# A transformer block's first loads: the eight norm columns by GpSimd's queue, the first x chunk by halves, its weights by ScalarE's queue, the table later, and a fixed order of two chunks

## The chip, the cores and the metric

The kernel runs on one core of one Trainium2 chip. The metric is the device time of one execution, in microseconds (us), as the median over executions. A profile of one more execution shows what each engine did: TensorE (PE, with PEld for its weight loads), VectorE (DVE), ScalarE (ACT), GpSimd (POOL), and SyncE (SP), which here only issues transfers. A "q" behind an engine's name is its instruction sequencer, which issues DMAs.

## What is computed

One block of a transformer on 512 tokens of width 1024, in float32. The parts that matter here:

```
h = rmsnorm(x, attn_pre_g)          # x * rsqrt(mean(x*x)) * g
proj = h @ w_in                     # split into q, k, v, gates of two attentions
k_cmp, v_cmp = compress_kv(...)     # two small MLPs on strided windows
o = [nsa_attention(...), swa_attention(..., sinks)]
x = x + rmsnorm(o @ w_o, attn_post_g)
h = rmsnorm(x, mlp_pre_g)
a, u = split(h @ w_gate_up);  y = (gelu(conv(a)) * u) @ w_down
x = x + rmsnorm(y, mlp_post_g)
x = x + (p @ w_ple) * sigmoid(x @ w_ple_gate)
```

## The kernel before

Tokens lie along the free dimension: x is kept transposed, as 8 chunks of 128 rows (features) by 512 columns (tokens). Each float32 product is made of three matmuls with operands that are split in a rounded high part and a rest, low part: high by high, high by low, low by high. So each weight and each activation is split first: ScalarE (or VectorE) makes the high part by a copy in the rounded type, VectorE subtracts it for the low part.

The program starts with `consts`: a table `cols` of 128 by 160 float32 (norm gains, convolution taps, sinks and more as columns) is loaded through ScalarE's DMA queue; small constants are set by GpSimd; a first activation loads ScalarE's function table; VectorE zeroes a tile, and TensorE runs `WARM` matmuls on it, which compute nothing that is used.

`load_x` then issues from SyncE's queue, chunk by chunk, x (256 KB) and the first weights `wv` (204 KB, 408 columns: three value projections and the gates). For each chunk ScalarE multiplies x with the norm gain, a column of the table, and rounds it to the high part (line 330); the high part of the weights is made on VectorE for chunk 0 (line 332) and on ScalarE for the others (line 334); VectorE makes both low parts (lines 335, 336); and the squares of x are summed on the side for the norm (lines 321 to 325), whose factor is applied after the products. These instructions carry `keep`, which holds them in the order of the program on their engine.

`v_natural` runs 96 matmuls on these: for each of 8 chunks and each of 4 blocks of 128 tokens the three terms, into four PSUM banks. x is the stationary operand (loaded as weights of TensorE), `wv` the moving one. Lines 356 to 358 are high by high, high by low and low by high. Behind them come the compress projections, which use the same x tiles.

`bias_tables` builds distance tables for the attentions; it also negates the eight sink columns of the table (line 295), long before they are used.

The order of instructions on an engine is laid out when the kernel is built, by a list scheduler that simulates the program and starts what is ready; `keep_in_program_order` fixes the order of marked instructions. Fillers (projections that are not urgent) are put between the steps of the attentions. Weight tiles rotate in few buffers: tag "wh" has 6, and the raw weights 2.

Of the kernel before, what the change touches and what calls it, by code (L numbers as in the profile page):

```python
# [26 lines left out]
C_GPRE, C_GPOST, C_GMLP, C_GMPOST = 0, 8, 16, 24  # L27
C_CW = 32
C_CB = C_CW + 3 * NFF
C_SINK = C_CB + NFF  # L30
# [18 lines left out]
HALF = [slice(h * H, (h + 1) * H) for h in range(2)]  # L49
# [3 lines left out]


FILL_STEP = 650.0
WARM = 9
RATES = [0.36, 0.36, 0.9, 0.6]
BORDER = {6: .36, 7: .7, 8: .9}
SIX = 4
# [5 lines left out]
class Block:  # L65
# [181 lines left out]
    def consts(self):  # L247
        nc, cp = self.nc, self.cp
        self.cols = cp.tile([P, NCOL], F32, name="cols")
        nc.scalar.dma_start(self.cols, self.io["cols"])  # L250
        self.ones = cp.tile([P, 1], F32, name="ones")
        nc.gpsimd.memset(self.ones, 1.0)
        self.mhalf = cp.tile([P, NQT], F32, name="mhalf")
        nc.gpsimd.memset(self.mhalf, -0.5)
        first = self.tiny([P, 1], "act")
        nc.scalar.activation(first, self.ones, AF.Copy)
        idle = self.s([P, T], F32R)
        nc.vector.memset(idle.bitcast(F32), 0.0)
        warm = self.ps("mm")
        for i in range(WARM):  # L260
            nc.tensor.matmul(warm, idle[:, 0:P], idle, start=True, stop=True)
        self.ident = cp.tile([P, P], F32, name="ident")
        nc.gpsimd.memset(self.ident, 1.0)
        nc.gpsimd.affine_select(out=self.ident, in_=self.ident, compare_op=ALU.is_equal, fill=0.0, base=0,
                                pattern=[[-1, P]], channel_multiplier=1)
# [4 lines left out]
    def bias_tables(self):  # L270

        self.phase = "biastables"
        nc = self.nc
        fr = nc.gpsimd.to_reg(BIG)
        it = self.s([P, T], I32)
        nc.gpsimd.iota(it, pattern=[[-1, T]], base=T - P, channel_multiplier=1)
        dist = self.u([P, 7 * P])
        self.dist = dist[:, :T]
        nc.vector.tensor_copy(self.dist, it)
        nc.gpsimd.affine_select(out=self.dist, in_=self.dist, compare_op=ALU.is_ge, fill=fr, base=T - P,  # L280
                                pattern=[[-1, T]], channel_multiplier=1)
# [12 lines left out]
        self.nsink = self.cp.tile([P, 8], F32, name="nsink")  # L294
        nc.vector.tensor_scalar(self.nsink, self.cols[:, C_SINK : C_SINK + 8], -1.0, None, op0=ALU.mult)
        self.qscale = self.cp.tile([P, 8], F32, name="qscale")
        for h in range(16):
            sl = SLOPES[8 + h if h < 8 else h - 8]
            nc.gpsimd.memset(self.qscale[h % 2 * 64 : h % 2 * 64 + 64, h // 2 : h // 2 + 1], -(HD ** -0.5) / sl)


    def load_x(self):
        self.phase = "loadx"
        nc = self.nc
        self.xg = []
        self.wv = []
        acc = self.s([P, T])
        keep = self.tc.keep_in_program_order
        raws = []
        for c in range(KC):  # L310
            if c % 2 == 0:
                x2 = self.u([P, 2, T], F32, "p")
            xt = x2[:, c % 2, :]
            keep(nc.sync.dma_start(xt, self.io["xT"][:, c, :]))
            wr = self.u([P, 408])
            keep(nc.sync.dma_start(wr, self.io["wv"][c]))
            raws.append((xt, wr))

        def squares(c):
            if c == 0:  # L320
                keep(nc.scalar.activation(acc, raws[0][0], AF.Square))
            else:
                sq = self.s([P, T])
                keep(nc.scalar.activation(sq, raws[c][0], AF.Square))
                keep(nc.vector.tensor_add(acc, acc, sq))

        for c, (xt, wr) in enumerate(raws):
            g = self.u([P, 2, T], F32R)
            hi, lo = (self.u([P, 408], F32R, "wh") for _ in range(2))
            keep(nc.scalar.activation(g[:, 0, :], xt, AF.Copy, scale=self.col(C_GPRE + c)))  # L330
            if c == 0:
                keep(nc.vector.tensor_copy(hi, wr))
            else:
                keep(nc.scalar.activation(hi, wr, AF.Copy))
            keep(nc.vector.tensor_sub(lo, wr, hi.bitcast(F32)))
            keep(nc.vector.scalar_tensor_tensor(g[:, 1, :], xt, self.col(C_GPRE + c), g[:, 0, :].bitcast(F32),
                                                op0=ALU.mult, op1=ALU.subtract))
            self.wv.append((hi, lo))
            self.xg.append(g)
            if c > 0:  # L340
                squares(c - 1)
        squares(KC - 1)
        self.xacc = acc

    def v_natural(self):
        self.phase = "vnatural"
        nc = self.nc
        NV = 408
        pv = [self.ps(t) for t in ("s", "s", "s", "o")]
        for c in range(KC):  # L350
            x = self.xg[c]
            hi, lo = self.wv[c]
            for tb in range(NQT):
                ts = slice(tb * P, (tb + 1) * P)
                o = pv[tb][:, :NV]
                nc.tensor.matmul(o, x[:, 0, ts], hi, start=c == 0, stop=False)
                nc.tensor.matmul(o, x[:, 0, ts], lo, start=False, stop=False)
                nc.tensor.matmul(o, x[:, 1, ts], hi, start=False, stop=c == KC - 1)
        self.r1c, self.r1b = self.rstd(self.xacc, "r1")
        self.vs = []  # L360
        self.gate = self.cp.tile([P, NQT, 24], F32, name="gate")
        for tb in range(NQT):
            v = self.s([P, T])
            nc.scalar.activation(v[:, :NV], pv[tb][:, :NV], AF.Copy, scale=self.r1c[:, tb : tb + 1])
            vt = self.u([P, 6, 2, HD], F32R)
            vv = v[:, : 6 * HD].rearrange("p (k d) -> p k d", k=6)
            nc.vector.tensor_copy(vt[:, :, 0, :], vv)
            nc.vector.tensor_sub(vt[:, :, 1, :], vv, vt[:, :, 0, :].bitcast(F32))
            self.vs.append(vt)
            e = self.tiny([P, 24], "ge")  # L370
# [838 lines left out]
```

## Time and profile before

| | us |
|---|---|
| median of 3 runs | 665.4 (665.25 to 665.5) |
| the profiled execution | 665.88 |
| its span, first to last instruction | 663.9 |

The span covers the instructions of the core; the profiled execution's own time is 2.0 us longer, and lies 0.48 us above the median. In the rows, times are microseconds from the start of the span unless marked ns, L330 is line 330 of the kernel, and "out<-in" names the tiles that an instruction writes and reads. The ends of matmuls are modelled: matmuls are pipelined, so the distance between the starts of two says more than their duration.

### The profile page before, as it was taken

The numbers are of one execution on the slowest core, as the hardware profiler recorded it, in microseconds if no ns is written. First come the engines' busy times: TensorE is split into PE (matmuls) and PEld (weight loads), VectorE is DVE, ScalarE is ACT, GpSimd is POOL, SyncE is SP. The second block draws the span as 40 slices with busy tenths as digits, with TensorE's granted clock in tenths as the row PEclk, the third lists the DMA queues.
The fourth block names the chain that finished last, engine by engine and source line by source line (L and its number), as shares of the span: only waits on it lengthen the run. The fifth ranks groups of instructions, "written<-read, shape, count | busy, mean of one in ns | idle before, by whom it ended". The sixth has DMA issues, their size and how long they took to land.

```text
span 663.9 us, 9247 instructions
## 1 busy us (share of the span) xinstructions
PE 656.2 (99%) x3297; PEld 552.9 (83%) x3297; DVE 399.8 (60%) x828; ACT 324.0 (49%) x602; POOL 168.3 (25%) x247
## 2 busy tenths in 40 slices
PE   9999999999999999999999999999999999999997
PEld 8988778888888888888888888888888888889986
DVE  7795887978856469586555555555542333323873
ACT  7454587978887566264333333333332223222351
POOL 1111597677486060021101010111100000001000
PEclk9999999999999999999999999999999999999999
DMA  8436621202273430112233333323323444332032
GB/s 301 169 109 202 187 65 48 59 22 66 63 231 141 136 128 31 65 64 96 95 97 99 100 102 96 106 98 98 96 87 88 119 132 129 88 95 88 3 111 80
DMA packets 25069, 69.55 MB, mean 105 GB/s; under 512 B 3136, under 2 KB 5184, under 8 KB 25024
## 3 DMA queue, kind: packets, MB, share of 16 engines
q1 hardware_dynamic: 24880, 68.89, 33.0%
q8 instruction: 26, 0.43, 0.3%
q14 instruction: 19, 0.16, 0.1%
q10 hardware_dynamic: 144, 0.08, 0.0%
HBM read 59.52 MB, written 2.10 MB: 93 GB/s over the span
## 4 chain that ended last, share of the span: by engine, by line
PE 93%; DVE 3%; ACT 2%; POOL 1%; issue 0%; DMA 0%; SPq 0%; ACTq 0%; DVEq 0%
PE mlpup_pss L145 4%; PE mlpup_pss L149 4%; PE mlpup_pss L148 4%; PE mlpup_psmm L145 3%; PE mlpup_pst L145 3%; PE mlpup_psmm L149 3%; PE mlpup_pst L149 3%; PE mlpup_pst L148 3%; PE mlpup_psmm L148 3%; PE mlpdown_pss L149 3%; PE mlpdown_pss L145 3%; PE mlpdown_pss L148 3%; PE nsa_pso L555 2%; PE nsa_pst L522 2%; PE mlpdown_psmm L145 2%; PE mlpdown_psmm L149 2%
## 5 line engine op out<-in xcount | busy, mean ns | idle before, releaser
L126 ACT ACTIVATE mlpup_wh<-mlpup_wr 128x1024 fp32r<-128x1024 f32 x38 | 40.3, 1061 | 78.6 <-PE mlpup_pss L148 43.3
L982 POOL TENSOR_TENSOR mlpup_s<-mlpup_s,r3b 128x512 f32<-128x512 f32 x22 | 29.5, 1343 | 186.8 <-ACT mlpup_s L981 186.8
L126 ACT ACTIVATE mlpdown_wh<-mlpdown_wr 128x1024 fp32r<-128x1024 f32 (+1 forms) x28 | 28.0, 1000 | 84.6 <-PE mlpdown_pss L148 30.1
L130 DVE TENSOR_TENSOR mlpdown_wh<-mlpdown_wr,mlpdown_wh 128x1024 fp32r<-128x1024 f32 (+1 forms) x28 | 32.8, 1170 | 60.2 <-ACT mlpdown_wh L126 60.2
L130 DVE TENSOR_TENSOR mlpup_wh<-mlpup_wr,mlpup_wh 128x1024 fp32r<-128x1024 f32 x38 | 47.0, 1238 | 5.1 <-ACT mlpup_wh L126 5.0
L145 PE MATMUL mlpup_pss<-r_u,mlpup_wh 128*128 128x512 f32 x120 | 46.8, 390 | 0.0
L148 PE MATMUL mlpup_pss<-r_u,mlpup_wh 128*128 128x512 f32 x120 | 46.7, 389 | 0.0
L149 PE MATMUL mlpup_pss<-r_u,mlpup_wh 128*128 128x512 f32 x120 | 46.7, 389 | 0.0
L545 POOL TENSOR_SCALAR nsa_u<-nsa_u,nsa_nrc,gate 128x512 f32<-128x512 f32 (+3 forms) x64 | 38.4, 613 | 16.9 <-DVE nsa_nrc L681 11.7
L647 ACT ACTIVATE nsa_u<-nsa_u,nsa_nnm 128x512 f32<-128x512 f32 (+3 forms) x64 | 35.4, 554 | 7.6 <-DVE nsa_nnm L640 7.4
L527 DVE TENSOR_TENSOR nsa_u<-nsa_pst,nsa_u 128x512 fp32r<-128x512 f32 (+1 forms) x43 | 29.4, 686 | 6.8 <-ACT nsa_u L524 6.5
L237 POOL TENSOR_TENSOR mlpdown_s<-mlpdown_s,mlpdown_s 128x512 f32<-128x512 f32 x6 | 7.8, 1302 | 100.3 <-ACT mlpdown_s L236 100.3
L130 POOL TENSOR_TENSOR fill_wh<-fill_wr,fill_wh 128x1024 fp32r<-128x1024 f32 (+2 forms) x14 | 26.9, 1924 | 24.1 <-ACT fill_wh L126 21.5
L975 DVE TENSOR_TENSOR mlpup_u<-mlpup_pss,r3b 128x512 f32<-128x512 f32 x17 | 11.7, 691 | 34.4 <-PE mlpup_pss L149 34.4
L981 ACT ACTIVATE mlpup_s<-mlpup_s 128x512 f32<-128x512 f32 x22 | 13.8, 632 | 37.7 <-DVE mlpup_s L980 37.6
L149 PE MATMUL mlpdown_pss<-mlpup_u,mlpdown_wh 128*128 128x512 f32 (+1 forms) x88 | 32.0, 364 | 0.0
L145 PE MATMUL mlpdown_pss<-mlpup_u,mlpdown_wh 128*128 128x512 f32 (+1 forms) x88 | 32.0, 364 | 0.0
L148 PE MATMUL mlpdown_pss<-mlpup_u,mlpdown_wh 128*128 128x512 f32 (+1 forms) x88 | 31.9, 363 | 0.0
L145 PE MATMUL mlpup_pst<-r_u,mlpup_wh 128*128 128x512 f32 x80 | 31.1, 389 | 0.0
L148 PE MATMUL mlpup_pst<-r_u,mlpup_wh 128*128 128x512 f32 x80 | 31.1, 389 | 0.0
L149 PE MATMUL mlpup_pst<-r_u,mlpup_wh 128*128 128x512 f32 x80 | 31.1, 389 | 0.0
L145 PE MATMUL mlpup_psmm<-r_u,mlpup_wh 128*128 128x512 f32 x80 | 31.1, 389 | 0.0
(426 smaller groups left out, 1988.1 us busy)
## 6 DMA issues: line engine op xcount, KB each, us to landing
mlpup_wr<-in_gu_dram SPq DMA_DIRECT2D x38, 512.0 KB, 3.3
mlpdown_wr<-in_down_dram SPq DMA_DIRECT2D x16, 512.0 KB, 3.6
fill_wr<-in_win_dram SPq DMA_DIRECT2D x6, 512.0 KB, 4.0
mlpdown_wr<-in_down_dram SPq DMA_DIRECT2D x8, 384.0 KB, 3.1
fill_u<-fill_u SPq DMA_DIRECT2D x20, 128.0 KB, 2.6
loadx_u<-in_xT_dram SPq DMA_DIRECT2D x8, 256.0 KB, 4.9
compress_u<-projk_u SPq DMA_DIRECT2D x16, 128.0 KB, 2.3
mlpdown_wr<-in_wpg_dram SPq DMA_DIRECT2D x4, 512.0 KB, 3.4
```

Source lines behind the costliest of these rows:

```text
L126: h = nc.scalar.activation(hi, raw, AF.Copy)
L130: l = eng.tensor_sub(lw, raw, hi.bitcast(F32))
L145: r = self.pin(mm(ps, hi, x[:, 0, :], start=start, stop=False))
L148: mm(ps, lo, x[:, 0, :], start=False, stop=False)
L149: mm(ps, hi, x[:, 1, :], start=False, stop=stop)
L522: self.att(nc.tensor.transpose(pt[:, r * P : (r + 1) * P], src, self.ident))
L527: nc.vector.tensor_sub(t[rs, part, :], pt[rs], t[rs, 0, :].bitcast(F32))
L545: self.nc.gpsimd.tensor_scalar(ap, ap, col, gate, op0=ALU.mult, op1=ALU.mult)
L555: self.att(nc.tensor.matmul(po, v, t[:, part, :], start=start, stop=stop))
L647: nc.scalar.activation(dst, dst, AF.Exp, bias=nm[:, r, b : b + 1], scale=-1.0, accum_out=sm[:, r, b : b + 1])
L981: nc.scalar.activation(c0, c0, AF.Gelu_apprx_tanh)
L982: nc.gpsimd.tensor_mul(c0, c0, self.r3)
```

## The change

The eight columns of the first norm get a tile of their own, `gpre`, which GpSimd's queue loads; the scaling of x reads it. The whole table is loaded from SyncE's queue, behind the weights of chunk 2. The weights of chunk 0 are loaded from ScalarE's queue, where the table was. The x of chunk 0 comes in two halves of 256 columns, and is scaled and split by halves. The sinks are negated by GpSimd and not by VectorE. The warm matmuls are 7 and not 9, on a zero tile of 128 columns that each reads four times. The V matmuls run by term and then by block, and those of the first two chunks are held in the order of the program.

```
--- before.py
+++ after.py
@@ -53,7 +53,7 @@
 
 
 FILL_STEP = 650.0
-WARM = 9
+WARM = 7
 RATES = [0.36, 0.36, 0.9, 0.6]
 BORDER = {6: .36, 7: .7, 8: .9}
 SIX = 4
@@ -247,18 +247,22 @@
     def consts(self):
         nc, cp = self.nc, self.cp
         self.cols = cp.tile([P, NCOL], F32, name="cols")
-        nc.scalar.dma_start(self.cols, self.io["cols"])
+        self.gpre = cp.tile([P, KC], F32, name="gpre")
+        nc.gpsimd.dma_start(self.gpre, self.io["cols"][:, C_GPRE : C_GPRE + KC])
         self.ones = cp.tile([P, 1], F32, name="ones")
         nc.gpsimd.memset(self.ones, 1.0)
         self.mhalf = cp.tile([P, NQT], F32, name="mhalf")
         nc.gpsimd.memset(self.mhalf, -0.5)
+        self.wv0 = self.u([P, 408])
+        nc.scalar.dma_start(self.wv0, self.io["wv"][0])
         first = self.tiny([P, 1], "act")
         nc.scalar.activation(first, self.ones, AF.Copy)
-        idle = self.s([P, T], F32R)
+        idle = self.s([P, P], F32R)
         nc.vector.memset(idle.bitcast(F32), 0.0)
         warm = self.ps("mm")
         for i in range(WARM):
-            nc.tensor.matmul(warm, idle[:, 0:P], idle, start=True, stop=True)
+            nc.tensor.matmul(warm.rearrange("p (a n) -> p a n", a=4), idle,
+                             idle[:, None, :].broadcast_to([P, 4, P]), start=True, stop=True)
         self.ident = cp.tile([P, P], F32, name="ident")
         nc.gpsimd.memset(self.ident, 1.0)
         nc.gpsimd.affine_select(out=self.ident, in_=self.ident, compare_op=ALU.is_equal, fill=0.0, base=0,
@@ -292,7 +296,7 @@
         nc.gpsimd.affine_select(out=self.rowok, in_=self.ones, compare_op=ALU.is_ge, fill=0.0, base=-31,
                                 pattern=[[0, 1]], channel_multiplier=1)
         self.nsink = self.cp.tile([P, 8], F32, name="nsink")
-        nc.vector.tensor_scalar(self.nsink, self.cols[:, C_SINK : C_SINK + 8], -1.0, None, op0=ALU.mult)
+        nc.gpsimd.tensor_scalar(self.nsink, self.cols[:, C_SINK : C_SINK + 8], -1.0, None, op0=ALU.mult)
         self.qscale = self.cp.tile([P, 8], F32, name="qscale")
         for h in range(16):
             sl = SLOPES[8 + h if h < 8 else h - 8]
@@ -311,9 +315,16 @@
             if c % 2 == 0:
                 x2 = self.u([P, 2, T], F32, "p")
             xt = x2[:, c % 2, :]
-            keep(nc.sync.dma_start(xt, self.io["xT"][:, c, :]))
-            wr = self.u([P, 408])
-            keep(nc.sync.dma_start(wr, self.io["wv"][c]))
+            if c == 0:
+                for ts in HALF:
+                    keep(nc.sync.dma_start(xt[:, ts], self.io["xT"][:, c, ts]))
+                wr = self.wv0
+            else:
+                keep(nc.sync.dma_start(xt, self.io["xT"][:, c, :]))
+                wr = self.u([P, 408])
+                keep(nc.sync.dma_start(wr, self.io["wv"][c]))
+            if c == 2:
+                keep(nc.sync.dma_start(self.cols, self.io["cols"]))
             raws.append((xt, wr))
 
         def squares(c):
@@ -327,14 +338,17 @@
         for c, (xt, wr) in enumerate(raws):
             g = self.u([P, 2, T], F32R)
             hi, lo = (self.u([P, 408], F32R, "wh") for _ in range(2))
-            keep(nc.scalar.activation(g[:, 0, :], xt, AF.Copy, scale=self.col(C_GPRE + c)))
+            parts = HALF if c == 0 else [slice(0, T)]
+            for ts in parts:
+                keep(nc.scalar.activation(g[:, 0, ts], xt[:, ts], AF.Copy, scale=self.gpre[:, c : c + 1]))
             if c == 0:
                 keep(nc.vector.tensor_copy(hi, wr))
             else:
                 keep(nc.scalar.activation(hi, wr, AF.Copy))
             keep(nc.vector.tensor_sub(lo, wr, hi.bitcast(F32)))
-            keep(nc.vector.scalar_tensor_tensor(g[:, 1, :], xt, self.col(C_GPRE + c), g[:, 0, :].bitcast(F32),
-                                                op0=ALU.mult, op1=ALU.subtract))
+            for ts in parts:
+                keep(nc.vector.scalar_tensor_tensor(g[:, 1, ts], xt[:, ts], self.gpre[:, c : c + 1], g[:, 0, ts].bitcast(F32),
+                                                    op0=ALU.mult, op1=ALU.subtract))
             self.wv.append((hi, lo))
             self.xg.append(g)
             if c > 0:
@@ -350,12 +364,12 @@
         for c in range(KC):
             x = self.xg[c]
             hi, lo = self.wv[c]
-            for tb in range(NQT):
-                ts = slice(tb * P, (tb + 1) * P)
-                o = pv[tb][:, :NV]
-                nc.tensor.matmul(o, x[:, 0, ts], hi, start=c == 0, stop=False)
-                nc.tensor.matmul(o, x[:, 0, ts], lo, start=False, stop=False)
-                nc.tensor.matmul(o, x[:, 1, ts], hi, start=False, stop=c == KC - 1)
+            for part, w in ((0, hi), (0, lo), (1, hi)):
+                for tb in range(NQT):
+                    r = nc.tensor.matmul(pv[tb][:, :NV], x[:, part, tb * P : (tb + 1) * P], w,
+                                         start=c == 0 and w is hi and part == 0, stop=c == KC - 1 and part == 1)
+                    if c < 2:
+                        self.tc.keep_in_program_order(r)
         self.r1c, self.r1b = self.rstd(self.xacc, "r1")
         self.vs = []
         self.gate = self.cp.tile([P, NQT, 24], F32, name="gate")
```

## Rows read from the trace of the kernel before

**Rows 1.** The profile's page: busy time, share of the span, instructions.
```profile
PE 656.2 (99%) x3297; PEld 552.9 (83%) x3297; DVE 399.8 (60%) x828; ACT 324.0 (49%) x602; POOL 168.3 (25%) x247
```

**Rows 2.** Stretches: PE, PEld, DVE, ACT, POOL busy (x), clock, DMA share, GB/s.
```profile
1.52:6.00 4.48, 4.48 (x11) 3.35 (x12) 1.66 (x5) 2.21 (x4) 2.22 (x17) 1.00 0.91 282
6.00:24.00 18.00, 18.00 (x97) 17.98 (x97) 15.58 (x24) 13.79 (x24) 0.00 (x0) 1.00 0.64 225
...
48.00:100.00 52.00, 50.77 (x258) 40.42 (x257) 37.75 (x134) 34.20 (x83) 27.42 (x37) 1.00 0.54 152
100.00:200.00 100.00, 99.18 (x572) 82.94 (x571) 76.81 (x282) 82.24 (x223) 71.76 (x123) 1.00 0.29 85
```

**Rows 3.** Waits of TensorE: the first and the second of seven.
```profile
PE x_psmm L261 <- DVE x_s L258: 1.5, 1, 1.5
PE nsa_pss L580 <- DVE nsa_nnm L640: 0.4, 1, 0.4
```

**Rows 4.** Timeline: start, us, engine, line, operation, out<-in, count [idle before <-releaser].
```profile
0.98 0.48 DVE L258 MEMSET x_s<- 128x512 f32 x1 [0.98 <-PEq L1199]
...
1.26 0.41 SPq L316 DMA_DIRECT2D loadx_u<-in_wv_dram  x1
...
1.48 0.27 DVE L506 MEMSET vc<- 128x256 f32 x1
...
1.52 4.21 PE L261 MATMUL x_psmm<-x_s 128*128 128x512 f32 x9 [1.52 <-DVE x_s L258]
...
2.54 0.20 ACT L256 ACTIVATE x_act<-ones 128x1 f32<-128x1 f32 x1
...
4.35 0.17 DVE L295 TENSOR_SCALAR nsink<-cols 128x8 f32<-128x8 f32 x1 [2.60 <-DMA cols<-in_cols_dram]
4.35 0.72 ACT L330 ACTIVATE loadx_u<-loadx_u,cols 128x512 fp32r<-128x512 f32 x1 [1.61 <-DMA cols<-in_cols_dram]
4.71 0.37 DVE L332 CAST loadx_u<-loadx_u 128x408 fp32r<-128x408 f32 x1 [0.19 <-DMA loadx_u<-in_wv_dram]
...
5.12 0.58 DVE L335 TENSOR_TENSOR loadx_u<-loadx_u,loadx_u 128x408 fp32r<-128x408 f32 x1
...
5.53 0.54 PE L356 MATMUL vnatural_pss<-loadx_u,loadx_u 128*128 128x408 f32 x1
5.62 0.74 DVE L336 SCALAR_TENSOR_TENSOR loadx_u<-loadx_u,cols,loadx_u 128x512 fp32r<-128x512 f32 x1
...
5.72 0.73 ACT L330 ACTIVATE loadx_u<-loadx_u,cols 128x512 fp32r<-128x512 f32 x1 [0.65 <-DMA loadx_u<-in_xT_dram]
...
5.87 0.59 PE L357 MATMUL vnatural_pss<-loadx_u,loadx_u 128*128 128x408 f32 x1
...
6.88 0.34 PE L356 MATMUL vnatural_pss<-loadx_u,loadx_u 128*128 128x408 f32 x1
...
7.05 0.34 PE L357 MATMUL vnatural_pss<-loadx_u,loadx_u 128*128 128x408 f32 x1
...
8.16 0.35 PE L358 MATMUL vnatural_pso<-loadx_u,loadx_u 128*128 128x408 f32 x1
```

**Rows 5.** DMA issues of 0.7 to 0.85, 3.6 to 3.7, all: KB each, landing.
```profile
loadx_u<-in_xT_dram SPq DMA_DIRECT2D x1, 256.0 KB, 3.4
cols<-in_cols_dram ACTq DMA_DIRECT2D x1, 80.0 KB, 3.5
...
loadx_u<-in_xT_dram SPq DMA_DIRECT2D x1, 256.0 KB, 5.0
...
out_dram<-plegate_s SPq DMA_DIRECT2D x2, 128.0 KB, 1.7
w<-in_w_dram SPq DMA_DIRECT2D x1, 96.0 KB, 5.8
```

**Rows 6.** DMA packets and bytes of the stretch from 2 to 3 us.
```profile
DMA packets 142, 0.20 MB, mean 200 GB/s; under 512 B 1, under 2 KB 64, under 8 KB 142
```

**Rows 7.** Waits of SyncE's queue in the first 30 us: one row.
```profile
SPq L316 <- DMA cols<-in_cols_dram: 0.3, 1, 0.3
```

More of the change, by code (lines that the diff above doesn't have):

```diff
@@ L55 @@
 FILL_STEP = 650.0
-WARM = 9
+WARM = 7
 RATES = [0.36, 0.36, 0.9, 0.6]
@@ L249, in consts @@
         self.cols = cp.tile([P, NCOL], F32, name="cols")
-        nc.scalar.dma_start(self.cols, self.io["cols"])
+        self.gpre = cp.tile([P, KC], F32, name="gpre")
+        nc.gpsimd.dma_start(self.gpre, self.io["cols"][:, C_GPRE : C_GPRE + KC])
         self.ones = cp.tile([P, 1], F32, name="ones")
@@ L254, in consts @@
         nc.gpsimd.memset(self.mhalf, -0.5)
+        self.wv0 = self.u([P, 408])
+        nc.scalar.dma_start(self.wv0, self.io["wv"][0])
         first = self.tiny([P, 1], "act")
         nc.scalar.activation(first, self.ones, AF.Copy)
-        idle = self.s([P, T], F32R)
+        idle = self.s([P, P], F32R)
         nc.vector.memset(idle.bitcast(F32), 0.0)
@@ L260, in consts @@
         for i in range(WARM):
-            nc.tensor.matmul(warm, idle[:, 0:P], idle, start=True, stop=True)
+            nc.tensor.matmul(warm.rearrange("p (a n) -> p a n", a=4), idle,
+                             idle[:, None, :].broadcast_to([P, 4, P]), start=True, stop=True)
         self.ident = cp.tile([P, P], F32, name="ident")
@@ L294, in bias_tables @@
         self.nsink = self.cp.tile([P, 8], F32, name="nsink")
-        nc.vector.tensor_scalar(self.nsink, self.cols[:, C_SINK : C_SINK + 8], -1.0, None, op0=ALU.mult)
+        nc.gpsimd.tensor_scalar(self.nsink, self.cols[:, C_SINK : C_SINK + 8], -1.0, None, op0=ALU.mult)
         self.qscale = self.cp.tile([P, 8], F32, name="qscale")
@@ L313, in load_x @@
             xt = x2[:, c % 2, :]
-            keep(nc.sync.dma_start(xt, self.io["xT"][:, c, :]))
-            wr = self.u([P, 408])
-            keep(nc.sync.dma_start(wr, self.io["wv"][c]))
+            if c == 0:
+                for ts in HALF:
+                    keep(nc.sync.dma_start(xt[:, ts], self.io["xT"][:, c, ts]))
+                wr = self.wv0
+            else:
+                keep(nc.sync.dma_start(xt, self.io["xT"][:, c, :]))
+                wr = self.u([P, 408])
+                keep(nc.sync.dma_start(wr, self.io["wv"][c]))
+            if c == 2:
+                keep(nc.sync.dma_start(self.cols, self.io["cols"]))
             raws.append((xt, wr))
@@ L329, in load_x @@
             hi, lo = (self.u([P, 408], F32R, "wh") for _ in range(2))
-            keep(nc.scalar.activation(g[:, 0, :], xt, AF.Copy, scale=self.col(C_GPRE + c)))
+            parts = HALF if c == 0 else [slice(0, T)]
+            for ts in parts:
+                keep(nc.scalar.activation(g[:, 0, ts], xt[:, ts], AF.Copy, scale=self.gpre[:, c : c + 1]))
             if c == 0:
@@ L335, in load_x @@
             keep(nc.vector.tensor_sub(lo, wr, hi.bitcast(F32)))
-            keep(nc.vector.scalar_tensor_tensor(g[:, 1, :], xt, self.col(C_GPRE + c), g[:, 0, :].bitcast(F32),
-                                                op0=ALU.mult, op1=ALU.subtract))
+            for ts in parts:
+                keep(nc.vector.scalar_tensor_tensor(g[:, 1, ts], xt[:, ts], self.gpre[:, c : c + 1], g[:, 0, ts].bitcast(F32),
+                                                    op0=ALU.mult, op1=ALU.subtract))
             self.wv.append((hi, lo))
@@ L352, in v_natural @@
             hi, lo = self.wv[c]
[L353 to L358, printed above, removed]
+            for part, w in ((0, hi), (0, lo), (1, hi)):
+                for tb in range(NQT):
+                    r = nc.tensor.matmul(pv[tb][:, :NV], x[:, part, tb * P : (tb + 1) * P], w,
+                                         start=c == 0 and w is hi and part == 0, stop=c == KC - 1 and part == 1)
+                    if c < 2:
+                        self.tc.keep_in_program_order(r)
         self.r1c, self.r1b = self.rstd(self.xacc, "r1")
```

## The prediction

> **What bounds the kernel now.** I read the page first. TensorE is busy 99% of the span, no other engine over 60% [rows 1]. Then the busy time by stretches: TensorE lacks 1.23 us of work between 48 and 100 and 0.82 us between 100 and 200, and is full from 1.52 to 24 [rows 2]. Of the 7.7 us that 656.2 lacks to 663.9, another 1.52 are ahead of its first matmul [rows 4], and the 4.1 left I put at the tail. The waits of TensorE in the whole program are its first one, 1.5 us on VectorE's memset, and six of 0.2 to 0.4 us [rows 3]. So what is won at the start is kept if the matmuls behind it just move up, and it is worth what the first stretch of matmuls is shortened by.
>
> The start is read from the timeline, row by row, since the page's shares say nothing here [rows 4]. VectorE fills the zero tile from 0.98 for 0.48 us. Nine warm matmuls run from 1.52, 4.21 us with the tail of the last. The first matmul with data starts at 5.53. It is held at two ends that meet: the nine warm ones take (5.53 - 1.52) / 9 = 0.446 us each, which is just up; and its x operand was ready only then: ScalarE scaled x chunk 0 from 4.35 to 5.07, and the matmul started 0.46 after that. ScalarE had waited for the norm table, and so had VectorE's sign change of the sinks at 4.35. VectorE's rounding of the first weights started at 4.71, when they had landed. Removing only one of the two ends would give nothing. The change moves both.
>
> The clock: the matmuls of 408 columns start 0.34 apart at 5.53 and 5.87, and 0.17 apart at 6.88 and 7.05 [rows 4]. So TensorE works at its 1.2 GHz level until about 6.9 and at 2.4 GHz after, while the granted-clock column reads 1.00 in both stretches [rows 2]; I go by the spacing. It had worked without a gap from 1.52.
>
> **The change part by part.**
>
> *Warm-up.* The zero tile shrinks from 128x512 to 128x128. Memsets of 512 and 256 columns took 0.48 and 0.27 us [rows 4], so 0.21 for 256 columns, and 0.27 - 0.10 = 0.17 for 128: the warm matmuls start 0.31 earlier, at 1.21. Seven at 0.446 take 3.12; they read the same 128 columns four times, which I cost as the 512 of before. They are over at 4.33 instead of 5.53. This is the floor for the first matmul with data.
>
> *The first x chunk.* It goes by halves of 128 KB, each with its own issue on SP. The whole chunk, 256 KB, landed 3.4 us after its issue at 0.8, so at 4.2; the table of 80 KB, on ScalarE's queue and issued with it, 3.5 us after, at 4.3 [rows 5]. How soon does a half land? From below: the shortest landing of 128 KB in the trace, a store of the output, is 1.7 us [rows 5], which is 2.5. From above: the half shares the DMA engines with the 204 KB of weights now issued at 0.80, together 332 KB, as chunk and table did (336 KB), and between 2 and 3 us only 0.20 MB moved [rows 6], so it may be no earlier than 4.3. I take 3.9: it starts ahead, and half its old bytes are enough. The first weights, issued at 0.80 instead of 1.26 [rows 4], land about 0.46 earlier than 4.7, at 4.25; 0.37 us of VectorE makes their high part, 4.62.
>
> The Trainium skill (DMA: Bandwidth & Descriptors, Issuing engines are not separate DMA queues) says that transfers of several issuing engines run on the same 16 DMA engines, and only the issuing time is saved. The trace agrees so far: two queues were open and 200 GB/s moved in 2 to 3 us. By it alone the weights would win the 0.46 us of one issue and the half chunk what its bytes are smaller.
>
> *The eight norm columns.* 4 KB by GpSimd's queue. No row of before shows a DMA issued by GpSimd. Below: the 1.7 us of [rows 5], landing at 2.5. Above: the slowest landing of a small one, 5.8 us for 96 KB, 6.6. The nearest row is the table itself, at 3.5 us with twenty times the bytes, so 4.3 at most if the queue is as good; I take no later than 3.9, so that x decides.
>
> *Scaling by halves.* ScalarE: 128x512 takes 0.72, 128x1 0.20 [rows 4], so a half 0.20 + 0.26 = 0.46; two cost 0.20 us more than one. It is hidden: ScalarE next waited 0.65 us for x chunk 1. VectorE's second term: 0.74 for 512 columns, 0.17 for a small one, so 0.46 for a half and 0.17 us more for two. The sign change (0.17) leaves VectorE, so its sum is unchanged.
>
> *First matmul with data.* 3.9 + 0.46 + 0.46 = 4.82, against 5.53: 0.71 us earlier. The weights' high part is there at 4.62. Bounds: 4.33 to 4.65 with the early landings (the warm-up or the weights then decide), 5.22 at 4.3, 7.5 at 6.6. The second block of four matmuls wants the low part of the weights, 0.58 later, 5.20; four matmuls of 0.34 from 4.82 last until 6.18, so it waits for nothing. Its third block wants the second term of x, ready by 5.20 + 0.92 = 6.12. Nothing.
>
> *What 0.71 us is worth.* If the clock still rises at about 6.9, the time won is at the lower level: 0.71 / 0.34 = 2.1 matmuls, which later cost (8.16 - 6.88) / 7 = 0.184 each [rows 4]: 0.39 us. If the rise moves up with the matmuls it is all of 0.71. I take 0.5, nearer the first, as the warm matmuls start only 0.31 earlier.
>
> *The rest of the loads.* SP issues two things ahead of x chunk 1, as before (half and half for chunk and weights), so chunk 1 is still issued third, and it landed at 5.72, when ScalarE had waited for it [rows 4]. The table is put behind the third chunk's weights: one SP issue (0.43) ahead of chunk 3. SP also waited once for the table's landing before it issued [rows 7]: the eighth DMA back must have landed. With the halves and the columns there are two more in the first eight, so chunk 3 may be issued about 1.0 us later than at 3.6, landing near 9.6 instead of 5.0 us after its issue, at 8.6 [rows 5]. TensorE takes 12 x 0.184 = 2.2 us a chunk, so it wants chunk 3 after 4.82 + about 2.9 + 4.4 = 12.1, and ScalarE and VectorE need about 1.8 us before. Hidden, with 0.7 us over; without cover it would cost 1.0. Later chunks stand better: TensorE was full in 6 to 24, VectorE busy 15.6 of 18 and ScalarE 13.8 [rows 2].
>
> *The sign change on GpSimd* waits for the table, some 5 us later than now; behind it stand GpSimd's memsets and the reciprocal root of the norm, which follows the V matmuls; from 6 to 24 GpSimd had nothing to do [rows 2]. Nothing.
>
> *The order.* Each chunk does 12 matmuls, as before, by term and then by block. For two chunks it is fixed. The trace of before already has all of chunk 0's twelve first: the last starts at 8.16 [rows 4], 2.6 us after the first, with no room for a thirteenth. So I cost it at nothing. What comes free earlier or later by it are weight buffers, and none of TensorE's waits is for weights [rows 3].
>
> **Sum.** 665.88 - 0.5 = 665.4 for the profiled execution; this lies 0.48 above the median of 665.4, so 664.9 for the median. Its span is 663.9, about 2 us of launch and end lie around it and don't change. Something under 0.2%, 1.33 us, can't be told from no change. Even the earliest start (4.33, 1.20 us) with a rise that moves along wins 0.18%.
>
> **Rivals.**
>
> *The clock rises later* (slower). The warm matmuls end at 4.33 and the first with data start at 4.82, or 5.2: a gap of 0.5 to 0.9 us which before didn't have, after 3.1 us of work instead of 4.0. In before the rise came 5.4 us after the first warm matmul. If it has to come that long after the first matmul with data, it is at 10.2 and not 6.9: 3.3 us at 0.34 instead of 0.184 a matmul, 3.3 x 0.46 = 1.5 us lost, less the 0.39: 666.5. It decides from a rise more than 0.85 us late. For it: the gap; against it: a gap of 0.5 us is short beside the 3.1 us of work. The Trainium skill (TensorE: Matmul & The Clock Gate, What's actually happening) says that the clock is throttled by default and that sustained work releases it. The spacing in [rows 4] agrees with the release; whether the gap counts no row shows.
>
> *The norm columns are late* (slower). At 6.6 the first matmul is at 7.5, 2.0 us later than before, of which at most 1.4 us are at the lower level: 0.6 + 0.8 = 1.4 us lost and perhaps the clock too, 666.8 or more. It decides once they land after about 4.6. The Trainium skill (DMA: Bandwidth & Descriptors, Specifications) gives the first byte of GpSimd's path about 1 us against 0.6 for SP's; an estimate by that is a landing 0.4 us later than on another queue, which leaves the columns under 4.3. No row here shows it.
>
> *Nothing is won*: half and columns land no earlier than 4.3, the first matmul is at 5.2, and 0.31 / 0.34 x 0.184 = 0.17 us are left: 665.2.
>
> *The order elsewhere moves.* Most instructions have no fixed order, and a start that shifts by half a microsecond can reorder fillers in attention. To win there are the 2.05 us of idle TensorE between 48 and 200 [rows 2], to lose about as much: 663.4 or 666.9.
>
> **How the numbers follow.** Forecast (start 0.3 to 1.2 us earlier, the clock much as it was, 664.2 to 665.2) 0.50; nothing won 0.16; clock late 0.12; columns late 0.05; order elsewhere 0.17, of which 0.10 for the better. Over 0.2% faster means below 664.07: most of the better order, and some of the forecast with a little of it: 0.20. Slower, above 666.73: parts of the clock, the columns and the worse order: 0.15. The rest, 0.65, is the same. The range of 663.8 to 666.6 leaves out about 0.1 at each end.
>
> **What would show it.** Right: warm matmuls from about 1.2; the first matmul with data between 4.3 and 5.2; ScalarE's first half waiting for x and not for the columns; spacing of 0.18 from about 6.5 to 6.9; the end of the V matmuls 0.5 us before 23.9. Wrong: ScalarE's first half waiting for the columns; a spacing of 0.34 after 7.5; a wait of TensorE at the third or fourth chunk; new idle stretches after 48.

## The result: 1% slower

The changed kernel takes 672.2 us (median of 4 runs, 671.4 to 672.7) against 665.4: a ratio of 1.0098, with an interval of 1.0085 to 1.011. I had forecast 664.9, no change that can be told. The profiled execution took 671.72 us, with a span of 669.9, so 6.0 us more span than before. (The medians differ by 6.8 us. The profiled execution of before lies 0.5 us above its median, that of the changed kernel 0.5 below its own; what follows is about the 6.0.) Two causes that have nothing to do with each other make it up: 2.2 us at the start, and 3.8 us spread over the matmuls that follow, 2.0 of them in the MLP's up-projection.

**The start.** The timeline of the changed kernel; where it answers to [rows 4], the operations are the same.

```profile
0.91 0.17 DVE L261 MEMSET x_s<- 128x128 f32 x1 [0.91 <-PEq L1213]
...
1.13 3.18 PE L264 MATMUL x_psmm<-x_s 128*128 128x512 f32 x7 [1.13 <-DVE x_s L261]
...
1.33 0.78 POOL L251 DMA_DIRECT2D gpre<-in_cols_dram  x1 [0.81 <-POOLq L1213]
...
4.18 0.37 DVE L345 CAST loadx_u<-x_u 128x408 fp32r<-128x408 f32 x1 [2.82 <-DMA x_u<-in_wv_dram]
...
6.14 1.52 ACT L343 ACTIVATE loadx_u<-loadx_u,gpre 128x256 fp32r<-128x256 f32 x3 [3.40 <-DMA gpre<-in_cols_dram]
...
6.70 0.89 PE L369 MATMUL vnatural_pss<-loadx_u,loadx_u 128*128 128x408 f32 x3 [2.40 <-ACT loadx_u L343]
...
8.75 0.54 PE L369 MATMUL vnatural_pso<-loadx_u,loadx_u 128*128 128x408 f32 x1
9.09 1.22 PE L369 MATMUL vnatural_pss<-loadx_u,loadx_u 128*128 128x408 f32 x3
```

Its DMA issues of 0.75 to 0.85, and the columns' at 1.33, with size and time to landing:

```profile
x_u<-in_wv_dram ACTq DMA_DIRECT2D x1, 204.0 KB, 3.3
loadx_u<-in_xT_dram SPq DMA_DIRECT2D x1, 128.0 KB, 3.1
...
gpre<-in_cols_dram POOLq DMA_DIRECT2D x1, 4.0 KB, 4.8
```

The first half chunk landed at 3.9 and the weights were in use at 4.18, as I had worked out (3.9 and 4.25). ScalarE had both the half and nothing to do; what it waited for were the eight norm columns, 4 KB, which GpSimd issued at 1.33 and which landed 4.8 us later. The first matmul with data starts at 6.70 and not at 5.53, and TensorE stands for 2.4 us ahead of it.

That gap then costs a second time. Stretches of the changed kernel, TensorE's busy time and count, granted clock, DMA share and GB/s:

```profile
4.40:6.70 2.30, 0.00 (x0) 1.00 0.92 249
6.70:7.40 0.70, 0.70 (x4) 0.99 0.95 302
7.40:10.40 3.00, 3.00 (x10) 0.50 1.02 381
10.40:11.20 0.80, 0.80 (x5) 0.75 1.06 373
11.20:14.00 2.80, 2.80 (x17) 1.00 1.05 351
```

The clock had risen to 2.4 GHz while the warm matmuls ran (the trace records the rise at 3.98, and two of the first four matmuls with data start 0.18 apart); after the gap it falls at 7.39 to 0.50, 1.2 GHz, until 10.80. (In a_pad below, which starts alike, no rise is recorded before 10.2.) The matmuls at 8.75 and 9.09 stand 0.34 apart. Before, 1.25 us of the V matmuls were at the lower level, from 5.53 to about 6.8; here it is 3.4 us. The sum: 6.70 - 5.53 = 1.17 us later, plus half of 3.4 - 1.25 = 1.1, makes 2.2. The last V matmul, before and after:

```profile
23.70 0.35 PE L358 MATMUL vnatural_pso<-loadx_u,loadx_u 128*128 128x408 f32 x1
```

```profile
26.11 0.35 PE L369 MATMUL vnatural_pso<-loadx_u,loadx_u 128*128 128x408 f32 x1
```

It starts 2.4 us later. About 0.15 are above the sum, and most of that belongs to the second cause: past the rise of the clock, the V matmuls too stand 186.7 ns apart and not 185.0.

The 1.25 us of before are one execution's. The nine profiles of the kernel before and of its variants below (b_) begin alike, and by their clock records the rise comes anywhere from 4.3 to 6.8 us; the one of before is the latest. So against another execution of before the clock's part could be up to 0.6 us larger, half of the 1.25.

**The rest.** TensorE is full, and yet what follows takes longer. One line of the MLP's up-projection in the view by tile, before and after: duration in ns (least, median, most), first and last start.

```profile
L145 PE MATMUL mlpup_pss<-r_u,mlpup_wh x120: 389/389/481, 273.9 to 486.0; 128*128 128x512 f32 x120
```

```profile
L145 PE MATMUL mlpup_pss<-r_u,mlpup_wh x120: 388/394/483, 277.4 to 491.5; 128*128 128x512 f32 x120
```

From the first to the last start it is 212.1 us before and 214.1 after, for the same matmuls in the same order: 1% slower. Taken from the starts of all 958 pairs of neighbours in this stage, three matmuls (one for each term) take 680.7 ns before and 687.3 after. Not each of them is slower: from the first to the second it is 226.7 ns before and 232.1 after, from the second to the third 226.9 and 226.0, from the third to the next first 227.1 and 229.2. Behind the V stage the order of all instructions of TensorE, VectorE, ScalarE and SyncE is the same in both programs, but for one compress matmul that changes places with the norm's. So in this stage it is neither a wait nor another order: the same matmuls take longer.

### The profile page after: what moved, and what is told of

The parts are those of the page before. It is cut to its first block, busy times and chain, and to the rows that moved or that the text cites. A ratio compares the mean times of both kernels' runs of the same rounds, so it can differ in the third digit from the quotient of the medians.

```text
span 669.9 us, 9252 instructions
## 1 busy us (share of the span) xinstructions
PE 659.9 (99%) x3295; PEld 553.4 (83%) x3295; DVE 398.8 (60%) x828; ACT 324.2 (48%) x603; POOL 169.0 (25%) x249
## 4 chain that ended last, share of the span: by engine, by line
PE 94%; DVE 2%; ACT 2%; POOL 1%; DMA 1%; issue 1%; DVEq 0%; ACTq 0%; POOLq 0%
PE mlpup_pss L145 4%; PE mlpup_pss L149 4%; PE mlpup_pss L148 4%; PE mlpup_psmm L145 3%; PE mlpup_pst L145 3%; PE mlpup_pst L149 3%; PE mlpup_psmm L149 3%; PE mlpup_psmm L148 3%; PE mlpup_pst L148 3%; PE mlpdown_pss L145 3%; PE mlpdown_pss L149 3%; PE mlpdown_pss L148 3%; PE nsa_pst L536 2%; PE vnatural_pss L369 2%; PE nsa_pso L569 2%; PE mlpdown_psmm L145 2%
## 5 line engine op out<-in xcount | busy, mean ns | idle before, releaser
L145 PE MATMUL mlpup_psmm<-r_u,mlpup_wh 128*128 128x512 f32 x80 | 31.5, 394 | 0.0
L145 PE MATMUL mlpup_pst<-r_u,mlpup_wh 128*128 128x512 f32 x80 | 31.5, 394 | 0.0
L149 PE MATMUL mlpup_pst<-r_u,mlpup_wh 128*128 128x512 f32 x80 | 31.4, 392 | 0.0
L149 PE MATMUL mlpup_psmm<-r_u,mlpup_wh 128*128 128x512 f32 x80 | 31.4, 392 | 0.0
```

The lines of the kernel that those rows point to most:

```text
L145: r = self.pin(mm(ps, hi, x[:, 0, :], start=start, stop=False))
L149: mm(ps, hi, x[:, 1, :], start=False, stop=stop)
```

## The experiments

The last column is the sum for three matmuls in the up-projection, from the starts as above.

| kernel | median, us | ratio to before (interval) | ns |
|---|---|---|---|
| before | 665.4 to 665.7 | | 680.7 |
| changed | 672.2 | 1.0098 (1.0085 to 1.011) | 687.3 |
| a_pad | 671.5 | 1.0085 (1.007 to 1.01) | 687.3 |
| b_shift | 665.66 | 1.0002 (0.9992 to 1.0011) | 680.7 |
| a_act | 669.52 | 1.0053 (1.0037 to 1.007) | 687.3 |
| a_warm | 672.24 | 1.0096 (1.0081 to 1.0111) | 687.3 |
| a_lay | 668.77 | 1.0045 (1.0031 to 1.0059) | 680.7 |
| a_act_lay | 666.68 | 1.0011 (1.0002 to 1.002) | 680.7 |
| b_gap192 | 669.45 | 1.0056 (1.0042 to 1.007) | 687.3 |
| a_lay_w12 | 666.38 | 1.0012 (1.0003 to 1.0021) | 680.7 |
| best_a | 665.06 | 0.9991 (0.9982 to 1.0) | 680.7 |
| best_b | 665.5 | 0.9995 (0.9986 to 1.0004) | 680.7 |

**First theory on the slower matmuls: all tiles moved by 32 bytes.** The new tile of 32 bytes per partition lies in front of all the others. Two kernels, one from each side. a_pad:

```
-        self.gpre = cp.tile([P, KC], F32, name="gpre")
+        self.gpre = cp.tile([P, 2 * KC], F32, name="gpre")
...
```

> The changed kernel with the tile of the norm columns made 64 bytes wide per partition and not 32, of which the first 32 are loaded, so that all tiles behind it lie at multiples of 64 bytes again, as before the change; the instructions and their order are the same as in the changed kernel. Theory (addresses: the tiles of activations and weights that moved by 32 bytes slow each matmul): the three matmuls of an MLP step go back from 687 ns to 681, and about 3.6 of the 6.0 us of the span are gone: 668.6, from 668.2 to 669.2, with the V matmuls still ending 2.4 us late. Rival (GpSimd's DMA queue, once used, or the late start itself slows TensorE for the rest of the program): 687 ns stay, 672.2. Rival (the loss is all of the late start and its clock): 672.2.

b_shift, in the kernel before:

```
         nc.scalar.dma_start(self.cols, self.io["cols"])
+        self.gap = cp.tile([P, 8], F32, name="gap")
```

> The kernel before with one unused tile of 32 bytes per partition put behind the table, so that all tiles behind it move by 32 bytes; instructions and order are those of before. Theory (addresses): the three matmuls of an MLP step go from 681 to 687 ns and the time to 669.0, from 668.5 to 669.8, with the V matmuls ending where they did or 0.2 us later. Rivals (GpSimd's queue or the late start): no change, 665.4.

Both say no: 687.3 ns stay in a_pad, 680.7 in b_shift. The theory fell. a_act, made for the start, also took two rivals away, since it has no DMA by GpSimd and no late start, and still 687.3 ns (its tile is 64 bytes wide, as in a_pad):

```
...
-        nc.gpsimd.dma_start(self.gpre, self.io["cols"][:, C_GPRE : C_GPRE + KC])
+        nc.scalar.dma_start(self.gpre[:, 0:KC], self.io["cols"][:, C_GPRE : C_GPRE + KC])
```

> As a_pad (64 bytes), and the norm columns by ScalarE's queue, ahead of the first weights. Theory (the columns are late because GpSimd issues them late and its transfer's packets wait behind those of the other queues): the columns land by about 3.9, before the first half of x is used at 4.1; the weights, one issue later, at 4.6, and the first matmul with data starts at about 5.0 and not 6.7; the V matmuls end 0.2 to 0.7 us before those of the kernel before: 664.9, from 664.5 to 665.4. Rival (a transfer of 32-byte rows is slow whoever issues it): columns after 5.5, first matmul after 6.0, 667 or more.

At the start it did what was expected. Its DMA of the columns and its first matmul with data:

```profile
0.80 0.41 ACTq L251 DMA_DIRECT2D gpre<-in_cols_dram  x1
...
3.18 0.51 ACT L343 ACTIVATE loadx_u<-loadx_u,gpre 128x256 fp32r<-128x256 f32 x1
...
4.90 1.36 PE L369 MATMUL vnatural_pss<-loadx_u,loadx_u 128*128 128x408 f32 x3 [0.43 <-DVE loadx_u L345]
```

The same 4 KB landed 2.4 us after the issue. The matmul now waits for the first weights (L345), and in the profiled execution the last V matmul starts at 23.62, 0.1 us before that of the kernel before. So its 669.52 is the slower matmuls almost alone.

**Second theory: where the two operands lie to each other.** The new kernel takes its first weights' tile (tag u) ahead of the first x tile (tag p). A tag stands for a set of equal buffers, its slots, and the pool lays the regions of its tags in the order in which they are first asked for: before it was p, u, then the split weights wh; now it is u, p, wh. A slot of p is 4128 bytes (its largest tile has 4 x 257 numbers, 4112 bytes) and there are six, 192 more than 6 x 4096. So activations and split weights, 0 bytes apart modulo 4096 before, are 192 apart now. These distances are worked out from the kernel's text; no view shows addresses. a_lay takes one p tile first; b_gap192 puts 192 unused bytes between u and wh in the kernel before.

```
+        self.x2 = self.u([P, 2, T], F32, "p")
         self.wv0 = self.u([P, 408])
...
-                x2 = self.u([P, 2, T], F32, "p")
+                x2 = self.x2 if c == 0 else self.u([P, 2, T], F32, "p")
```

> The changed kernel with one x tile (tag p) taken from the pool ahead of the first weights' tile (tag u), as in the kernel before, so that the pool lays the regions of its tags in the old order, and the activations and the split weights are again the same number of bytes apart modulo 4096 (0, where the changed kernel has 192); instructions and order are those of the changed kernel. What fell: that all tiles moved by 32 bytes slows the matmuls (b_shift 665.66 with 681 ns for three matmuls, a_pad 671.5 with 687). Theory (where the moving operand and the stationary operand of TensorE lie to each other decides the spacing): 681 ns for the three matmuls of an MLP step, 668.2, from 667.6 to 668.8. Rival (something else in the changed program, such as the two warm matmuls less or the instructions' places): 687 ns, 672.

```
             wr = self.u([P, 408])
+            if c == 0:
+                self.gap = self.up.tile([P, 48], F32, tag="gap", name="gap", bufs=1)
```

> The kernel before with an unused tile of 192 bytes per partition in the pool between the region of the activations (tag u) and that of the split weights (tag wh), so that the two are 192 bytes apart modulo 4096, as in the changed kernel; instructions and order are those of before. Theory (places of the two operands to each other): 687 ns for the three matmuls and 669.5, from 668.9 to 670.1. Rival: no change, 665.5.

Both agree: a_lay has 680.7 ns again, b_gap192 687.3, and 3.9 us more than the kernel before run beside it (665.52), with nothing else changed. Their rows for the line shown above, a_lay and b_gap192:

```profile
L145 PE MATMUL mlpup_pss<-r_u,mlpup_wh x120: 389/389/481, 276.4 to 488.5; 128*128 128x512 f32 x120
```

```profile
L145 PE MATMUL mlpup_pss<-r_u,mlpup_wh x120: 388/394/482, 274.7 to 488.8; 128*128 128x512 f32 x120
```

**Which distances cost.** The gap of b_gap192 in other sizes, one run each.

> The kernel before with the two regions 512 bytes apart modulo 4096 and not 0 (b_gap192: 192, 687 ns for three matmuls, 669.45). Theory (any distance but 0 costs, and 512, the bytes of one row of a stationary tile, least): between 681 and 684 ns, 665.5 to 667.5. Rival (only the distance modulo 64 or 128 counts, and 192 was bad by chance): 681 ns exactly. Rival (every distance costs the same): 687 ns, 669.5.

> The kernel before with the two regions 64 bytes apart. Theory (any distance that is no multiple of 512 bytes costs about the same): 686 to 688 ns for three matmuls, 669.5. Rival (the cost grows with the distance): 681 to 684 ns. Rival (only distances that are an odd multiple of 64 cost): 687 ns, and b_gap128 681.

> 128 bytes apart. Theory (no multiple of 512): 686 to 688 ns, 669.5. Rival (multiples of 128 are free): 681 ns, 665.5.

> 256 bytes apart. Theory (no multiple of 512): 686 to 688 ns, 669.5. Rival (multiples of 256 are free): 681 ns, 665.5.

> 704 = 512 + 192 bytes apart. Theory (the distance counts modulo 512): the 687 ns and 669.45 of b_gap192. Rival (a large distance is free): 681 ns, 665.5.

| bytes apart | 0 | 64 | 128 | 192 | 256 | 512 | 704 |
|---|---|---|---|---|---|---|---|
| three matmuls, ns | 680.7 | 700.5 | 700.4 | 687.3 | 680.7 | 680.7 | 687.3 |
| one run, us (192: median of 4) | 665.7 | 676.09 | 676.05 | 669.45 | 665.59 | 665.35 | 669.54 |

My theory for these, a period of 512, was wrong: 256 is free. All seven agree with a distance that counts modulo 256: 0, 256 and 512 are free, 192 and 704 = 2 x 256 + 192 cost the same, and 64 and 128 cost three times that. b_gap64 from the first to the last start of the line:

```profile
L145 PE MATMUL mlpup_pss<-r_u,mlpup_wh x120: 393/394/478, 276.2 to 494.4; 128*128 128x512 f32 x120
```

218.2 us and not 212.1. It is the distance that counts and not where the weights lie by themselves: in a_act_lay and best_a below, the tile of 64 bytes moves activations and weights together by 64, and three matmuls take 680.7 ns; b_gap64 moves the weights, and what lies behind them, but not the activations, and they take 700.5. Distances of less than 64 weren't tried, nor the same on tiles other than these.

**The gap and the clock.** a_warm fills the gap with warm matmuls (`WARM = 13`), and a_lay_w12 does so with 12 and the old layout.

> As a_pad (64 bytes), with 13 warm matmuls and not 7, which last until the late norm columns are used, about 6.8. Theory (the late columns cost 1.2 us of start, and the gap ahead of it another 1.2 us by a clock that rises at 10.8 and not at 6.8): the spacing of the V matmuls is 0.18 from about 7.0 at the latest, they end 0.8 to 1.2 us later than in the kernel before and not 2.4, and the time is 1.2 to 1.5 us under that of a_pad: 667.3, from 666.9 to 667.8. Rival (the clock's rise doesn't depend on the gap): as a_pad within 0.4 us.

> As a_lay, with 12 warm matmuls and not 7, which last until about 6.4, near the use of the late norm columns; the order of all other instructions is that of a_lay (with 13, in a_warm, the order of the norm's small matmuls behind the V matmuls had changed too, and cost more than was won). Theory (the gap ahead of the first data holds the clock down until about 10.8): the V matmuls end 1.2 to 1.8 us before those of a_lay, and the time is 1.2 to 1.8 us under it: 666.7. Rival (the gap doesn't matter for the clock): as a_lay within 0.4 us.

In a_warm the V matmuls end 1.7 us sooner than in a_pad, and the whole is no faster. The waits of its TensorE tell why:

```profile
PE projk_psmm L145 <- DVE compress_s L443: 1.2, 1, 1.2
```

With 13 warm matmuls the list scheduler had put the norm's eight small matmuls behind eleven of compress; the norm came 0.9 us later than in a_pad, and what needs it held TensorE up. So a_warm doesn't tell the theories apart. a_lay_w12, whose order is that of a_lay, does: 2.4 us under a_lay, more than the 1.2 to 1.8 expected. In its profile the warm matmuls last until 5.6 and the first with data starts at 6.68, as in the changed kernel, and goes at 0.18 a matmul from there on:

```profile
6.68 0.85 PE L370 MATMUL vnatural_pss<-loadx_u,loadx_u 128*128 128x408 f32 x3 [1.08 <-ACT loadx_u L344]
7.37 0.34 PE L370 MATMUL vnatural_pso<-loadx_u,loadx_u 128*128 128x408 f32 x1
7.55 0.72 PE L370 MATMUL vnatural_pss<-loadx_u,loadx_u 128*128 128x408 f32 x3
8.11 0.34 PE L370 MATMUL vnatural_pso<-loadx_u,loadx_u 128*128 128x408 f32 x1
```

So the five warm matmuls more keep the clock, across a gap of 1.1 us; the ten runs lie between 666.0 and 666.7, so not in the profiled execution alone.

**Late columns and layout both undone.** a_act_lay is a_act with the edit of a_lay; best_a has 9 warm matmuls as well; best_b issues the columns behind the weights.

> As a_lay, with the norm columns by ScalarE's queue ahead of the first weights (a tile of 64 bytes, as in a_act). Theory (the late columns and the layout are all of the loss): the time of a_act less 4.0 us, 665.4, from 664.9 to 665.8; the V matmuls end 0.3 us before those of the kernel before. Rival: layout is not the cause, 669.5.

> As a_act_lay (old layout, norm columns by ScalarE's queue ahead of the first weights), with 9 warm matmuls and not 7, which last from 1.13 to 5.14, so that no gap is left ahead of the first matmul with data. What a_act and a_act_lay showed: both start that matmul at 4.9 to 5.0, and the spacing falls to 0.18 at 6.9 in the one and at 10.9 in the other, and a_act_lay's times spread from 665.3 to 667.6. Theory (with a gap the clock's rise is late in some executions): the spread closes, all runs between 664.9 and 665.7, and the median is 665.2, 0.3 us under the kernel before. Rival (the late rise has nothing to do with the gap): the spread stays, median 666.5.

> As best_a, with the norm columns on ScalarE's queue behind the first weights. Theory (the weights, issued 0.41 us earlier, were what the first matmul waited for; the columns, 2.4 us from issue to landing in a_act, are still in time at 3.7): the first matmul with data at 5.1, held by the warm ones alone, as in best_a; 665.2, from 664.9 to 665.6. Rival (columns land behind the weights, after 4.3): first matmul at 5.3 and a small gap, 665.2 to 666.5 with a spread.

a_act_lay missed its 665.4. Its first matmul starts at 5.00, as in a_act, but in the profiled execution the clock stays low until 10.8:

```profile
7.52 0.54 PE L370 MATMUL vnatural_pso<-loadx_u,loadx_u 128*128 128x408 f32 x1
7.86 1.22 PE L370 MATMUL vnatural_pss<-loadx_u,loadx_u 128*128 128x408 f32 x3
8.88 0.54 PE L370 MATMUL vnatural_pso<-loadx_u,loadx_u 128*128 128x408 f32 x1
...
10.58 0.80 PE L370 MATMUL vnatural_pss<-loadx_u,loadx_u 128*128 128x408 f32 x3
11.22 0.35 PE L370 MATMUL vnatural_pso<-loadx_u,loadx_u 128*128 128x408 f32 x1
```

In a_act, with the same start and nearly the same gap, it rose at 6.9:

```profile
6.40 0.95 PE L369 MATMUL vnatural_pss<-loadx_u,loadx_u 128*128 128x408 f32 x3
7.19 0.35 PE L369 MATMUL vnatural_pso<-loadx_u,loadx_u 128*128 128x408 f32 x1
7.38 0.72 PE L369 MATMUL vnatural_pss<-loadx_u,loadx_u 128*128 128x408 f32 x3
```

The times of a_act_lay go from 665.3 to 667.6 (one run of 812 us stands apart). With 9 warm matmuls, which leave no gap, the spread is 664.8 to 666.1 and the median 1.6 us lower. That is the late clock as I had described it, but as a matter of chance from one execution to the next and not of the kernel. The profiles together agree: of the five kernels with 7 warm matmuls only a_act is at 2.4 GHz for good by 7 us, the others rise for good at 10.2 to 11.2; of the eleven with 9, all are by 6.8. best_a closes the gap and adds two warm matmuls at once, so which of the two it is, no run tells.

best_a is the fastest version: 665.06, 0.09% under the kernel before, with an interval that just reaches 1. In the profiled execution it starts its V stage at 5.13, and its last V matmul, at 23.26, is 0.4 us earlier than before. All of that goes again: a wait that the kernel before didn't have in its profile, for the copies of the keys, stands in best_a's list and in those of b_shift (1.4) and b_late (1.5), whose V stages ended 0.4 us early too. best_a's wait, and its first and last start in the up-projection:

```profile
PE nsa_pss L596 <- DMA compress_u<-projk_u: 1.2, 1, 1.2
```

```profile
L145 PE MATMUL mlpup_pss<-r_u,mlpup_wh x120: 389/389/481, 274.3 to 486.3; 128*128 128x512 f32 x120
```

The kernel before started there at 273.9, so in this execution nothing of the 0.4 us was kept.

best_b is no better, since behind the weights the columns landed only at 4.7.

**GpSimd's queue by itself.** b_late loads the same rows once more, at a quiet moment of the kernel before.

```
+        late = self.tiny([P, KC], "late", bufs=1)
+        nc.scalar.activation(late, self.xg[KC - 1][:, 0, 0:KC].bitcast(F32), AF.Copy)
+        nc.gpsimd.dma_start(late, self.io["cols"][:, C_GPRE : C_GPRE + KC])
```

> The kernel before, with the same 128 rows of 32 bytes loaded once more by GpSimd's queue at about 16.8, when the other queues are nearly idle, into a tile that nothing reads (a small copy on ScalarE of the last x chunk into it sets the moment). Theory (in the changed kernel its packets waited behind the other queues' in the DMA engines): it lands within 3.0 us of its issue. Rival (GpSimd's path takes that long by itself): 4.5 us or more, as at the start (4.8). The time says nothing here.

Its view by tile: duration in ns (786) and start (16.8) of the issue, and the time to landing.

```profile
L345 POOL DMA_DIRECT2D loadx_late<-in_cols_dram x1: 786/786/786, 16.8 to 16.8; - x1
...
DMA to landing us min/median/max: 3.1/3.1/3.1
```

3.1 us, a little over the 3.0 of the theory and far from the 4.5 of the rival. So of the 6.1 us at which the columns were there in the changed kernel, 0.5 are an issue that begins at 1.33 and not at 0.8, 3.1 are the queue by itself (2.4 on ScalarE's queue, at a busy moment), and 1.7 come on top at the start, with the other loads under way. That it is these loads, and not GpSimd's own next instructions, no run shows apart. The changed kernel's packets of GpSimd's queue by stretches, 3.5 to 4.5, 4.5 to 5.5 and 5.5 to 6.2:

```profile
q0 software_dynamic: 24, 0.00, 13.9%
...
q0 software_dynamic: 2, 0.00, 0.1%
...
q0 software_dynamic: 1, 0.00, 0.1%
```

Of 32 packets three came after 4.5, the last at 5.81, and the transfer counts as landed only behind it, at 6.1. By the trace the three hold 4 bytes each; the sixteen packets of 256 bytes, which are the data, had all begun by 4.04.

## Why the prediction was wrong

*Warm-up*: right. Memset 0.17 us, warm matmuls from 1.13 (I had 1.21), over at 4.3.

*First x chunk, first weights, scaling by halves, VectorE's part*: right to 0.1 us, but covered by the next.

*The eight norm columns*: the step that failed at the start. I took "no later than 3.9, so that x decides"; they landed at 6.1. The bound of 6.6 and the rival that they are late were there, with a price of 1.4 us and a chance of 0.05. The rows gave no GpSimd DMA, and I filled in the row of another queue, with twenty times the bytes. The bytes were not what counts. The price was low as well, 2.2 us for a landing at 6.1 where I had 1.4 "and perhaps the clock too" for one at 6.6, since the late columns and the late clock, two rivals in my list, come together here: the one makes a gap ahead of the other. The Trainium skill (DMA: Bandwidth & Descriptors, Specifications) puts the first byte at about 1 us on GpSimd's path and 0.6 on SP's, 0.4 us apart by estimate. To landing this case shows 3.1 us on GpSimd's queue in quiet and 2.4 on ScalarE's at a busier moment, not far from that, but 4.8 on GpSimd's among other loads, which those figures don't tell.

*What the start is worth*: the mechanism was right (the time at 1.2 GHz costs half), the sign of its term wrong: 0.5 us to be won, 2.2 lost. The clock rival had the rise at 10.2; it was 10.8. I had counted it from the first warm matmul, 5.4 us by the one profile that I had; in the nine profiles that begin alike it comes 2.8 to 5.3 us after it, so the 5.4 was one draw and no fixed delay. The Trainium skill (TensorE: Matmul & The Clock Gate, What's actually happening) has the clock throttled by default and released by activity. The trace agrees as far as that goes: the granted clock rose at 3.98 under the warm matmuls, and read 0.50 from 7.39 on, behind a gap of 2.4 us. The row that the prediction said was missing, whether a shorter gap counts, is now there twice, with two answers: a_act kept its rise at 6.9 after a gap of 0.4 us, a_act_lay with one of 0.5 us did not.

*The rest of the loads, the sign change, the order*: right at nothing. The V matmuls wait for no later chunk, and the order behind them stayed, but for one compress matmul.

*What isn't in the prediction at all*: 3.8 of the 6.0 us. I put the new tile and the earlier allocation of the first weights' tile at nothing, without noticing them as edits. No view of the profile of before shows addresses. The line that fails is "what is won at the start is kept if the matmuls behind it just move up": they took longer, 1% on average in the up-projection. b_gap192 shows the size by itself, 3.9 us, and a_lay takes 3.4 back (668.77 against 672.21). The line fails in best_a too, in another way: there the matmuls move up, and a wait for the keys' copies takes the gain. What in the chip makes TensorE slower when its stationary and its moving operand lie at other distances modulo 256 was not tried; the runs show that they do and by how much.

Together: late columns and clock 2.2 us and layout 3.8 make 6.0 of span. The parts of the change that do what they say are worth 0.6 us at most (best_a, 665.06 against 665.67 for the kernel before run beside it, an interval that reaches no gain), and with 9 warm matmuls, not 7.

## What to carry to other kernels

The order in which tiles are first taken from a pool is part of the schedule: after an edit that moves an allocation, compare the spacing of matmuls far from the edit before looking for a wait; here activations and split weights at a multiple of 256 bytes from each other took 680.7 ns for three matmuls, and 64 bytes off 700.5. A small transfer that starts a chain should go on a queue whose latency a trace has shown, and be there well ahead: bytes don't set its price, 4 KB took 2.4 us on one queue, 3.4 on the same queue behind 204 KB (best_b), and 4.8 on another. Warm matmuls should reach up to the first real one: with two fewer the clock rose for good at 10.2 us or later in four profiles of five, and with nine at 6.8 at the latest. And a gain at the start is a gain only if nothing later waits for something else: look for the wait that it will meet.

## What the runs showed of the hardware

- The time of a matmul with its own weight load depends on the distance of its two operands in a partition, with a period that fits 256 bytes in all seven distances tried: 226.9 ns at 0, 256 and 512, 229.1 at 192 and 704, 233.5 at 64 and 128 (128x512, float32r; from start to start, mean of the three terms). Moving both by 32 bytes (b_shift, a_lay) or by 64 (a_act_lay, best_a) changed nothing.
- A 4 KB load (128 rows of 32 bytes) landed 2.4 us after its issue on ScalarE's queue and 3.4 when issued behind 204 KB there; on GpSimd's, 3.1 us in quiet and 4.5 to 4.8 in five profiles with SyncE's and ScalarE's loads under way, where the last packets to come held 4 bytes each.
- After a gap of 2.4 us the granted clock fell from 1.0 to 0.50 at 7.4 us, 0.7 us after the matmuls had begun again, and stayed there until 10.8. With 7 warm matmuls and gaps of about half a microsecond the rise came at 6.9 in one execution and at 10.8 in another. With 9 it came from 4.3 to 6.8 in the nine profiles of the kernel before and its variants.
